# Transposing the gated feed-forward activations between the next pairs of k-tiles, and reloading the spilled ones through another pool of tiles

## The chip, the cores and the metric

The kernel is one program on one core of one Trainium2 chip. The metric is the device time of a whole execution in microseconds (us), the median of several runs. Engines are named as the profile names them: PE is TensorE (matrix products and transposes) and PEld its weight loads, DVE is VectorE, ACT is ScalarE, POOL is GpSimd, and SP is the engine that issues nearly all transfers (DMA).

## What is computed

The reference is one transformer layer on 256 positions of 2048 features, in fp32. Three kinds of attention come first; the part that matters here is the feed-forward block and what stands on either side of it:

```
h = layer_norm(ALPHA * h + mixed @ w_out[i], ln1_g[i], ln1_b[i])
a, b = jnp.split(h @ w_ffn_in[i], 2, axis=-1)
h = layer_norm(ALPHA * h + (jax.nn.silu(a) * b) @ w_ffn_out[i], ln2_g[i], ln2_b[i])
```

Here `h` is 256 x 2048, `w_ffn_in` is 2048 x 11264 (so `a` and `b` have 5632 columns each), and `w_ffn_out` is 5632 x 2048. `silu(a) * b` are the gated activations.

## The kernel before

**Products.** To keep fp32 accuracy each operand is split into a high part and a low remainder (`halves`, L144 on ACT for the high part, L145 on DVE for the low one), and each product is three matmuls: high by high, low by high, high by low. Weights come from HBM in tiles of 512 KB (two k-tiles of 128 rows by 512 columns), are split into `whi` and `wlo`, and feed PE. The 256 positions are two halves of 128, `h` = 0 and 1.

**The gated chunks.** The 5632 columns of the gate are 11 chunks of 512, `c` = 0 to 10. Chunk 0 (`first_chunk`) runs two plain products (`gemm`, matmul lines L212 to L214). Chunks 1 to 10 (`next_chunk`) go through `pair_gemm` (matmul lines L257 to L259), which handles the 16 k-tiles as eight pairs p0 to p7; a plain pair is 24 matmuls. Pairs 2 and 4 (`SEVEN`) use a seven-product form of a 2x2 block product, which needs combinations of the activations that `Forms.put` prepares (L233 to L238, `xs`, `xf`), and four more PSUM banks `m[1]`, `m[5]`, `m[6]`, `m[7]`, used in the order 1, 7, 5, 6. PSUM has two pools of four banks, `acc` and `sc`; a chunk's sums `c[h][j]` take one (`own`), its `m` tiles the other, and the next chunk swaps them. A chunk ends with additions from PSUM (L307), `silu` on ACT (L951) and the multiplication by `b` on DVE (L952; L945 for chunk 0) into a `g` tile, of which pool `gp` has three.

**Transposing.** The next product needs the activations with features on the partitions. `keep_act` calls `to_dmajor` for each half: four PE transposes of 128x128 into one PSUM bank (L335), emptied by ACT (L966), or by ACT and DVE with the split (L144, L145). Chunks 0 and 1 stay on chip (`STAY` is 2). Chunks 2 to 10 go to an HBM buffer `actd` (L968) and come back in `act_first` (L986) while the first column tile of `w_ffn_out` is computed: the load lands in a tile of pool `raw`, is split into two `k4` tiles, and serves four k-tiles. The pool `raw` has three buffers, and the plain products' weight loads (L155) use the same three.

**What sets the order.** The functions are written as Python that emits instructions; a scheduler then decides each engine's own order, so that it need not be the order of the code. Each engine works through its own list strictly in that order, and waits on semaphores. Beside the main stream there is a list of side tasks: generators that `add` puts there and that `tick` moves on by one step. `gemm` and `pair_gemm` call `tick` after each group of weights or pair. A step's `yield n` asks for `n` ticks until the next.

Of the kernel before, what the change touches and what calls it, by code (L numbers as in the profile page):

```python
# [10 lines left out]
F32 = mybir.dt.float32  # L11
# [4 lines left out]
P = 128  # L16
S = 256
# [16 lines left out]
STAY, AHEAD = 2, 1  # L34
# [87 lines left out]
def build(ctx: ExitStack, tc: tile.TileContext, A: dict):  # L122
    nc = tc.nc
    PE, DVE, ACT, POOL = nc.tensor, nc.vector, nc.scalar, nc.gpsimd

    keep = ctx.enter_context(tc.tile_pool(name="keep", bufs=1))
    wp = ctx.enter_context(tc.tile_pool(name="wp", bufs=4))
    k4 = ctx.enter_context(tc.tile_pool(name="k4", bufs=16))
# [13 lines left out]
    def halves(src, hi, lo):  # L142

        ACT.activation(hi, src, AF.Copy)  # L144
        DVE.tensor_sub(lo, src, hi.bitcast(F32))  # L145
# [16 lines left out]
    side, now, newest = [], [0], [None]  # L162

    def add(gen, *after):
        task = {"gen": gen, "after": after, "done": False, "at": 0}
        side.append(task)
        return task
# [11 lines left out]
    def gemm(src, X, kt, w, sizes=(), spare=(), between=None, parts=1):  # L179

        ps = [acc_tile() for _ in range(1 + parts)]
        cols = [[(ps[0][:, :w], slice(0, w))], []]
        for i in range(parts):
            cols[1].append((ps[1 + i][:, :w // parts], slice(i * w // parts, (i + 1) * w // parts)))
        nk = 1
        while nk * 2 * w <= 1024 and nk < 8:
            nk *= 2  # L190
        rest, at = list(sizes), 0
        while at < kt:
            W = []
            sizes = rest.pop(0) if rest else [nk]
            many = len(sizes) > 4
            for g, n in enumerate(sizes):
                n = min(n, kt - at)
                pool = spare[g] if many and g < len(spare) else None
                hi, lo = weight_group(src[:, at:at + n, :], n, w, pool)
                W.append((at, n, hi, lo))  # L200
                at += n
            newest[0] = lo
            for half in range(2):
                if half and not rest and at == kt and between:
                    between(ps)
                c = slice(half * P, (half + 1) * P)
                for o, d in cols[half]:
                    for k0, n, hi, lo in W:
                        for k in range(k0, k0 + n):
                            xh, xl = X(k)  # L210
                            h, l = hi[:, k - k0, d], lo[:, k - k0, d]
                            PE.matmul(o, xh[:, c], h, start=(k == 0), stop=False)  # L212
                            PE.matmul(o, xl[:, c], h, start=False, stop=False)  # L213
                            PE.matmul(o, xh[:, c], l, start=False, stop=(k == kt - 1))  # L214
            tick()
        return ps
# [27 lines left out]

    def pair_gemm(a, b, X, F, kt, pool, banks):

# [5 lines left out]
        hs = [slice(0, P), slice(P, S)]  # L252
        np_, last = kt // 2, max(F.at)

        def product(o, x, w, first=False, stop=False):
            (xh, xl), (h, l) = x, w
            PE.matmul(o, xh, h, start=first, stop=False)  # L257
            PE.matmul(o, xl, h, start=False, stop=False)  # L258
            PE.matmul(o, xh, l, start=False, stop=stop)  # L259

        def split(src, name, pool, n, **kw):
            hi, lo = (pool.tile([P, n, 512], F32R, name=f"w{name}{x}", tag=f"w{name}{x}", **kw) for x in ("hi", "lo"))
            halves(src, hi, lo)
            return [(hi[:, i, :], lo[:, i, :]) for i in range(n)]

        for p in range(np_):
# [3 lines left out]
            x = [[tuple(t[:, hs[h]] for t in X(2 * p + k)) for k in range(2)] for h in range(2)]  # L270
            if p not in F.at:
                w = [split(raw[:, 2:4, :], "", wp, 2), split(raw[:, 0:2, :], "", wp, 2)]
# [18 lines left out]
            product(c[0][0], x[0][1], b21)  # L291
            product(c[0][1], F(p, 3), b22)
            product(m[7], F(p, 2), t3, first, stop)
            product(m[5], F(p, 0), t1, first, stop)
            product(m[6], F(p, 1), t2, first, stop)
# [35 lines left out]
    def to_dmajor(X, k0, src, half, raw=None, bank=None):  # L331

        tp = (bank or sc_tile)()
        for i in range(4):
            PE.transpose(tp[:, i * P:(i + 1) * P], src[:, i * P:(i + 1) * P], ident)  # L335
        tp = tp.rearrange("p (n t) -> p n t", n=4)
        if X is not None:
            X.put(k0, 4, half, tp)
        if raw is not None:
            raw(half, k0, tp)  # L340

    def g_tile():
        return gp.tile([P, 2, 512], F32, name="g", tag="g")
# [480 lines left out]
    dram = ctx.enter_context(tc.tile_pool(name="dram", bufs=9, space=bass.MemoryType.DRAM))  # L824
# [4 lines left out]
    for n in range(4):  # L829
        G = gates(n) if n else G0  # L830
        mix = None
        for name, kt, k0 in (("dsa", 6, 10), ("nsa", 4, 0), ("fox", 6, 4)):
            ps = gemm(A["br_" + name][n], lambda k: O(k0 + k), kt, 512)
            g = G[name]
# [101 lines left out]
    actT = Halves()  # L936

    def first_chunk():
        g = g_tile()
        ps = gemm(A["ffn_in"][0], hT, KT, 512, sizes=[[2] * LONG3], spare=[k4b] * (LONG3 - 4))  # L940
        for h in range(2):
            ACT.activation(g[:, h, :], ps[h], AF.Silu)
        ps = gemm(A["ffn_in"][11], hT, KT, 512)
        for h in range(2):
            DVE.tensor_mul(g[:, h, :], g[:, h, :], ps[h])  # L945
        return [g[:, h, :] for h in range(2)]

    def next_chunk(c, pool, banks):
        e = pair_gemm(A["ffn_in"][c], A["ffn_in"][11 + c], hT, F, KT, pool, banks)
        for h in range(2):  # L950
            ACT.activation(e[h][:, 0, :], e[h][:, 0, :], AF.Silu)  # L951
            DVE.tensor_mul(e[h][:, 0, :], e[h][:, 0, :], e[h][:, 1, :])  # L952
        return [e[h][:, 0, :] for h in range(2)]

    spilled = {}

    def keep_act(c, g, bank):

        if c < STAY:
            actT.add(k4)  # L960
            for h in range(2):
                to_dmajor(actT, 4 * c, g[h], h, bank=bank)
            return
        t = k4.tile([P, 4, S], F32, name="act", tag="k4")
        for h in range(2):
            to_dmajor(None, 4 * c, g[h], h, lambda h, k0, tp: ACT.copy(t[:, :, h * P:(h + 1) * P], tp), bank)  # L966
        spilled[c] = dram.tile([P, 4, S], F32, name="actd")
        nc.sync.dma_start(spilled[c], t)  # L968

    keep_act(0, first_chunk(), acc_tile)  # L970
    part.close()
    with tc.tile_pool(name="fw", bufs=2) as fw:
        F = Forms(k4, SEVEN)
        for p in SEVEN:
            F.put(p, hT)
        for c in range(1, 11):
            banks = (sc_tile, acc_tile) if c % 2 else (acc_tile, sc_tile)
            keep_act(c, next_chunk(c, fw, banks), banks[0])
    k4b = ctx.enter_context(tc.tile_pool(name="k4c", bufs=14))

    def act_first(k):

        for c in range(len(actT.t), min(k // 4 + AHEAD + 1, 11)):
            raw = wp.tile([P, 1024], F32, name="raw", bufs=3)
            raw = raw.rearrange("p (k t) -> p k t", k=4)
            nc.sync.dma_start(raw, spilled[c])  # L986
            actT.add(k4 if c < 4 else k4b)
            halves(raw, *actT.t[c])
        return actT(k)

    later = Later(k4)
    add_and_norm(A["ffn_out"], actT, 44, lambda n: (Y[0][n], Y[1][n]), lambda: params("ln2_g", "ln2_b", k4),
                 lambda: gated_input(k4, 2, k4), later, LONG2, [k4b] * (LONG2 - 4), first=act_first)
    h2T = later.x
    for n in range(4):
# [61 lines left out]
```

## Time and profile before

| what | value |
|---|---|
| median of 3 runs | 1626.53 us (1626.1 to 1627.22) |
| time of the profiled execution | 1622.71 us |
| its span, first to last instruction | 1620.4 us |
| PE busy | 1600.4 us (99%), 7521 matmuls and transposes |
| DVE busy | 1036.8 us (64%) |
| ACT busy | 770.1 us (48%) |
| mean granted TensorE clock | 0.998 |
| bytes moved | 319.71 MB, mean 197 GB/s |

The span is what the trace covers; the profiled execution's own time is 2.3 us longer, for what lies around it, and 3.8 us under the median of the runs. The ends of matmuls are modelled in the trace, so a PE that is shown busy may still be running below its pace; starts of successive matmuls are the better measure.

### The profile page before, as it was taken

To read this page: it belongs to the slowest core of one execution; us is meant where nothing else is said; L and a number is where in the kernel's file an instruction comes from. 1 tells how busy PE (TensorE), PEld (TensorE's weight loads), DVE (VectorE), ACT (ScalarE), POOL (GpSimd) and SP (SyncE) were. 2 spreads that over 40 slices of the span, in tenths; PEclk is the share of its full clock that TensorE was granted. 3 is DMA by queue.
4 is the path that set the end of the run, shared out by engine and by line. 5 is a ranking of instruction groups with operands and counts; after the bars stand their busy time and mean duration, and the time that the engine had idled before them with its cause. 6 is when DMAs were issued, how large, how long until landed. Compare 5 with 4: busy or idle time off the path is not lost. (4 is left out here: it accounts for less than half of the span.)

```text
span 1620.4 us, 19963 instructions
## 1 busy us (share of the span) xinstructions
PE 1600.4 (99%) x7521; PEld 1337.9 (83%) x7521; DVE 1036.8 (64%) x1346; ACT 770.1 (48%) x958; POOL 17.9 (1%) x38
## 2 busy tenths in 40 slices
PE   9999999999999999999999999999999999999998
PEld 7777899988888888888878888888888778888787
DVE  5679765554646454566777777777878555545764
ACT  5455555554444444444455545445555444433443
POOL 1000000010000000000000000000000000000000
PEclk9999999999999999999999999999999999999999
DMA  8665653566666666677565556656566677666474
GB/s 264 191 194 154 206 159 110 167 207 227 189 193 190 194 192 186 194 233 224 163 214 183 192 203 219 211 205 209 207 221 235 201 236 222 193 194 196 152 232 132
DMA packets 92752, 319.71 MB, mean 197 GB/s; under 512 B 10608, under 2 KB 11760, under 8 KB 92656
## 3 DMA queue, kind: packets, MB, share of 16 engines
q1 hardware_dynamic: 91376, 314.25, 61.2%
q0 software_dynamic: 1280, 4.20, 0.9%
q8 instruction: 59, 0.97, 0.2%
q14 instruction: 37, 0.30, 0.1%
HBM read 311.58 MB, written 6.82 MB: 196 GB/s over the span
## 5 line engine op out<-in xcount | busy, mean ns | idle before, releaser
L145 DVE TENSOR_TENSOR wlo<-raw,whi 128x1024 fp32r<-128x1024 f32 (+2 forms) x532 | 633.1, 1193 | 504.6 <-ACT whi L144 499.0
L144 ACT ACTIVATE whi<-raw 128x1024 fp32r<-128x1024 f32 (+2 forms) x532 | 550.4, 1035 | 722.8 <-PE acc L213 372.7
L212 PE MATMUL acc<-whi,k4h 128*128 128x512 f32 (+3 forms) x1580 | 608.3, 385 | 2.1 <-ACT k4h L144 1.6
L214 PE MATMUL acc<-wlo,k4h 128*128 128x512 f32 (+3 forms) x1580 | 602.1, 381 | 3.2 <-DVE wlo L145 3.2
L213 PE MATMUL acc<-whi,k4l 128*128 128x512 f32 (+3 forms) x1580 | 602.0, 381 | 0.6 <-DVE k4l L145 0.6
L212 PEld LDWEIGHTS acc<-whi,k4h 128*128 128x128 f32 x1580 | 297.7, 189 | 56.9 <-ACT k4h L144 2.4
L214 PEld LDWEIGHTS acc<-wlo,k4h 128*128 128x128 f32 x1580 | 297.6, 188 | 56.8 <-DVE wlo L145 5.2
L213 PEld LDWEIGHTS acc<-whi,k4l 128*128 128x128 f32 x1580 | 297.9, 189 | 51.6 <-DVE k4l L145 1.4
L259 PE MATMUL acc<-wlo,k4h 128*128 128x512 f32 x240 | 94.4, 393 | 0.0
L259 PE MATMUL sc<-wlo,k4h 128*128 128x512 f32 x240 | 94.2, 393 | 0.0
L258 PE MATMUL acc<-whi,k4l 128*128 128x512 f32 x240 | 93.6, 390 | 0.0
L257 PE MATMUL sc<-whi,k4h 128*128 128x512 f32 x240 | 93.5, 390 | 0.0
L258 PE MATMUL sc<-whi,k4l 128*128 128x512 f32 x240 | 93.5, 390 | 0.0
L257 PE MATMUL acc<-whi,k4h 128*128 128x512 f32 x240 | 93.5, 389 | 0.0
L258 PEld LDWEIGHTS acc<-whi,k4l 128*128 128x128 f32 x240 | 45.1, 188 | 9.5
L258 PEld LDWEIGHTS sc<-whi,k4l 128*128 128x128 f32 x240 | 45.1, 188 | 9.4
L257 PEld LDWEIGHTS sc<-whi,k4h 128*128 128x128 f32 x240 | 45.1, 188 | 9.1
L259 PEld LDWEIGHTS sc<-wlo,k4h 128*128 128x128 f32 x240 | 45.1, 188 | 9.1
L257 PEld LDWEIGHTS acc<-whi,k4h 128*128 128x128 f32 x240 | 45.1, 188 | 9.1
L259 PEld LDWEIGHTS acc<-wlo,k4h 128*128 128x128 f32 x240 | 45.1, 188 | 9.0
L145 DVE TENSOR_TENSOR wtlo<-raw,wthi 128x1024 fp32r<-128x1024 f32 x40 | 47.9, 1220 | 0.0
L144 ACT ACTIVATE wthi<-raw 128x1024 fp32r<-128x1024 f32 x40 | 41.2, 1046 | 2.4 <-DVE raw L282 2.0
(305 smaller groups left out, 1208.5 us busy)
## 6 DMA issues: line engine op xcount, KB each, us to landing
raw<-ffn_in SPq DMA_DIRECT2D x176, 512.0 KB, 4.5
raw<-gate SPq DMA_DIRECT2D x96, 512.0 KB, 3.6
raw<-ffn_out SPq DMA_DIRECT2D x88, 512.0 KB, 4.3
raw<-att_c SPq DMA_DIRECT2D x40, 512.0 KB, 4.4
raw<-att_f SPq DMA_DIRECT2D x48, 384.0 KB, 3.3
raw<-w_out SPq DMA_DIRECT2D x32, 512.0 KB, 3.7
raw<-ple_gate SPq DMA_DIRECT2D x32, 512.0 KB, 4.4
raw<-cmp SPq DMA_DIRECT2D x16, 512.0 KB, 4.1
```

Of the source, the lines that this page charges most:

```text
L144: ACT.activation(hi, src, AF.Copy)
L145: DVE.tensor_sub(lo, src, hi.bitcast(F32))
L212: PE.matmul(o, xh[:, c], h, start=(k == 0), stop=False)
L213: PE.matmul(o, xl[:, c], h, start=False, stop=False)
L214: PE.matmul(o, xh[:, c], l, start=False, stop=(k == kt - 1))
L257: PE.matmul(o, xh, h, start=first, stop=False)
L258: PE.matmul(o, xl, h, start=False, stop=False)
L259: PE.matmul(o, xh, l, start=False, stop=stop)
```

## The change

`keep_act` becomes a generator with one step for each half. `on_the_side` runs it up to its first `yield` at once (which takes the tiles) and hands the rest to the side list, so that the first half's transposes are emitted at the first `tick` after it, and the second half's at the next. Chunk 0's task is handed over once `F` is made, and `F.put` follows it in the code. The spilled chunks come back into a `g` tile of pool `gp`, not a `raw` tile.

```diff
     def keep_act(c, g, bank):
         if c < STAY:
             actT.add(k4)
-            for h in range(2):
-                to_dmajor(actT, 4 * c, g[h], h, bank=bank)
-            return
-        t = k4.tile([P, 4, S], F32, name="act", tag="k4")
+            put, done = actT, None
+        else:
+            t = k4.tile([P, 4, S], F32, name="act", tag="k4")
+            put, done = None, lambda h, k0, tp: ACT.copy(t[:, :, h * P:(h + 1) * P], tp)
         for h in range(2):
-            to_dmajor(None, 4 * c, g[h], h, lambda h, k0, tp: ACT.copy(t[:, :, h * P:(h + 1) * P], tp), bank)
-        spilled[c] = dram.tile([P, 4, S], F32, name="actd")
-        nc.sync.dma_start(spilled[c], t)
-
-    keep_act(0, first_chunk(), acc_tile)
+            yield 1
+            to_dmajor(put, 4 * c, g[h], h, done, bank)
+        if c >= STAY:
+            spilled[c] = dram.tile([P, 4, S], F32, name="actd")
+            nc.sync.dma_start(spilled[c], t)
+
+    def on_the_side(gen):
+        add(gen)["at"] = now[0] + next(gen)
+
+    g = first_chunk()
     part.close()
     with tc.tile_pool(name="fw", bufs=2) as fw:
         F = Forms(k4, SEVEN)
+        on_the_side(keep_act(0, g, acc_tile))
         for p in SEVEN:
             F.put(p, hT)
         for c in range(1, 11):
             banks = (sc_tile, acc_tile) if c % 2 else (acc_tile, sc_tile)
-            keep_act(c, next_chunk(c, fw, banks), banks[0])
+            on_the_side(keep_act(c, next_chunk(c, fw, banks), banks[0]))
...
-            raw = wp.tile([P, 1024], F32, name="raw", bufs=3)
-            raw = raw.rearrange("p (k t) -> p k t", k=4)
+            raw = g_tile().rearrange("p h (k t) -> p (h k) t", t=S)
             nc.sync.dma_start(raw, spilled[c])
```

First place, PE at the end of chunk 0 and the start of chunk 1. Before, the eight transposes stand after the first product of chunk 1 (the `sc<-whi` rows are its pair p0):

```order
L214 MATMUL acc<-wlo,k4h 128x512
L257 MATMUL sc<-whi,k4h 128x512
L258 MATMUL sc<-whi,k4l 128x512
L259 MATMUL sc<-wlo,k4h 128x512
L335 MATMUL acc<-ident,g 128x128 x8
L257 MATMUL sc<-whi,k4h 128x512
```

With the change four of them stand after the 24 matmuls of pair p0, and the other four after the 24 of pair p1, ahead of the seven-product pair p2 (`wdhi`); the piece shown is the second:

```order
L259 MATMUL sc<-wlo,k4h 128x512
L335 MATMUL acc<-ident,g 128x128 x4
L257 MATMUL acc<-wdhi,k4h 128x512
L258 MATMUL acc<-wdhi,k4l 128x512
L259 MATMUL acc<-wdlo,k4h 128x512
L257 MATMUL sc<-wdhi,k4h 128x512
```

So both sets move behind one and two pairs of independent products. In chunks 2 to 10 both sets stood inside pair p0 before (four transposes, then nine matmuls, then four), and move in the same way.

Second place, PE at the end of chunk 10, where the first column tile of `w_ffn_out` begins (L212 to L214). Before, all eight transposes stand ahead of its first matmul:

```order
L259 MATMUL acc<-wlo,k4h 128x512
L335 MATMUL acc<-ident,g 128x128 x8
L212 MATMUL acc<-whi,k4h 128x512
L213 MATMUL acc<-whi,k4l 128x512
L214 MATMUL acc<-wlo,k4h 128x512
```

With the change the first four stand after the first 12 matmuls of that product (one weight tile), and the second four, shown here with the end of the first 12 ahead of the first four, after 12 more:

```order
L214 MATMUL acc<-wlo,k4h 128x512
L335 MATMUL acc<-ident,g 128x128 x4
L212 MATMUL acc<-whi,k4h 128x512
L213 MATMUL acc<-whi,k4l 128x512
L214 MATMUL acc<-wlo,k4h 128x512
```

Third place, SP's list in the same stretch: `raw<-ffn_out` are weight tiles, `actd<-act` is the last store, and the loads from `actd` bring chunks 2, 3, 4, ... back. Before:

```order
L155 DMA raw<-ffn_out 128x1024 x2
L870 DMA g<-pT 128x512
L986 DMA raw<-actd 128x1024
L155 DMA raw<-ffn_out 128x1024 x2
L986 DMA raw<-actd 128x1024
L155 DMA raw<-ffn_out 128x1024
L968 DMA actd<-act 128x1024
L155 DMA raw<-ffn_out 128x1024
L986 DMA raw<-actd 128x1024
L155 DMA raw<-ffn_out 128x1024 x2
```

With the change:

```order
L155 DMA raw<-ffn_out 128x1024 x2
L992 DMA g<-actd 128x1024
L155 DMA raw<-ffn_out 128x1024 x4
L992 DMA g<-actd 128x1024
L155 DMA raw<-ffn_out 128x1024
L971 DMA actd<-act 128x1024
L992 DMA g<-actd 128x1024
L155 DMA raw<-ffn_out 128x1024
L992 DMA g<-actd 128x1024
L155 DMA raw<-ffn_out 128x1024 x2
```

The loads of spilled chunks no longer stand between the weight loads as users of the same three buffers, and the last store stands ahead of the load of chunk 4 and the ninth weight tile.

ACT's list at the start of chunk 3 shows what the copies of chunk 2's transposes stand behind. Before (`whi_7759` belongs to pair p1, `whi_7835` and `whi_7839` to p3, `whi_7918` to p5, `wthi` to p2):

```order
L144 ACTIVATE whi_7759<-raw8_7752 128x1024
L966 COPY act_7698<-acc_7699 128x4x128
L966 COPY act_7698<-acc_7705 128x4x128
L144 ACTIVATE whi_7835<-raw8_7832 128x1024
L144 ACTIVATE whi_7839<-raw8_7832 128x1024
L144 ACTIVATE wthi_7803<-raw_7791 128x1024
```

With the change:

```order
L144 ACTIVATE whi_7835<-raw8_7832 128x1024
L144 ACTIVATE whi_7839<-raw8_7832 128x1024
L965 COPY act_7698<-acc_7738 128x4x128
L144 ACTIVATE wthi_7803<-raw_7791 128x1024
L965 COPY act_7698<-acc_7779 128x4x128
L144 ACTIVATE whi_7918<-raw8_7915 128x1024
```

Both copies move behind the weights of p3 and stay ahead of those of p5. In chunk 1 alone the second half's copy (`k4h`) moves behind the weights of p5 as well.

## Rows read from the trace of the kernel before

**Rows 1.** The page, busy us, share of the span and instructions by engine:
```profile
PE 1600.4 (99%) x7521; PEld 1337.9 (83%) x7521; DVE 1036.8 (64%) x1346; ACT 770.1 (48%) x958; POOL 17.9 (1%) x38
```

**Rows 2.** Waits of PE, whole span: us in total, times, longest:
```profile
PE acc L335 <- DVE g L952: 3.5, 1, 3.5
PE acc L214 <- DVE wlo L145: 3.2, 3, 2.1
PE acc L335 <- DVE g L945: 2.0, 1, 2.0
```

**Rows 3.** Timeline of PE, chunk 0 to chunk 1: start, us, instruction [idle before]:
```profile
835.66 0.39 PE L259 MATMUL sc<-wlo,k4h 128*128 128x512 f32 x1
838.07 1.25 PE L335 MATMUL acc<-ident,g 128*128 128x128 f32 x8 [2.02 <-DVE g L945]
839.08 0.48 PE L257 MATMUL sc<-whi,k4h 128*128 128x512 f32 x1
```

**Rows 4.** Timeline of PE, chunk 10 to the first product of `w_ffn_out`:
```profile
1269.21 0.39 PE L259 MATMUL acc<-wlo,k4h 128*128 128x512 f32 x1
...
1273.51 0.66 PE L335 MATMUL acc<-ident,g 128*128 128x128 f32 x4 [3.47 <-DVE g L952]
1273.92 0.47 PE L212 MATMUL acc<-whi,k4h 128*128 128x512 f32 x1
...
1278.11 0.39 PE L214 MATMUL acc<-wlo,k4h 128*128 128x512 f32 x1
```

**Rows 5.** Windows: us, busy us by engine, granted clock (after POOL), DMA share, GB/s:
```profile
838.00:840.00 2.00, 1.93 (x12) 1.63 (x13) 2.00 (x4) 1.20 (x2) 0.00 (x0) 1.00 1.02 410
1273.00:1278.00 5.00, 4.49 (x15) 3.63 (x16) 2.22 (x3) 1.67 (x3) 0.00 (x0) 0.66 0.74 188
```

**Rows 6.** Timeline of PE late in the first column tile of `w_ffn_out`:
```profile
1321.68 0.39 PE L214 MATMUL acc<-wlo,k4h 128*128 128x512 f32 x1
...
1323.11 0.50 PE L214 MATMUL acc<-wlo,k4h 128*128 128x512 f32 x1 [0.53 <-DVE wlo L145]
...
1329.83 0.50 PE L214 MATMUL acc<-wlo,k4h 128*128 128x512 f32 x1 [0.53 <-DVE wlo L145]
...
1330.40 0.39 PE L213 MATMUL acc<-whi,k4l 128*128 128x512 f32 x1
```

**Rows 7.** Timeline of SP, two successive loads of spilled chunks:
```profile
1294.38 0.33 SPq L986 DMA_DIRECT2D raw<-actd  x1
...
1301.25 0.33 SPq L986 DMA_DIRECT2D raw<-actd  x1
```

**Rows 8.** DMA issues, 1270 to 1323 us: KB each, median us to landing:
```profile
raw<-ffn_out SPq DMA_DIRECT2D x15, 512.0 KB, 4.2
raw<-actd SPq DMA_DIRECT2D x8, 512.0 KB, 4.3
```

**Rows 9.** Timeline of PE at an ordinary boundary, chunk 2 to chunk 3:
```profile
967.20 0.39 PE L258 MATMUL acc<-whi,k4l 128*128 128x512 f32 x1
...
968.14 0.39 PE L257 MATMUL acc<-whi,k4h 128*128 128x512 f32 x1
...
969.98 0.60 PE L335 MATMUL sc<-ident,g 128*128 128x128 f32 x4
...
975.00 0.39 PE L258 MATMUL acc<-whi,k4l 128*128 128x512 f32 x1
...
978.63 0.39 PE L259 MATMUL acc<-wlo,k4h 128*128 128x512 f32 x1
```

**Rows 10.** Timeline of ACT in chunk 3:
```profile
970.62 0.59 ACT L966 COPY act<-sc 128x512 f32<-128x512 f32 x1 [1.03 <-PE sc L335]
...
981.66 1.06 ACT L144 ACTIVATE whi<-raw 128x1024 fp32r<-128x1024 f32 x1 [6.21 <-DMA raw<-ffn_in]
```

**Rows 11.** DMA issues, 800 to 822 us, in chunk 0:
```profile
raw<-ffn_in SPq DMA_DIRECT2D x15, 512.0 KB, 5.5
```

**Rows 12.** Windows, 800 to 820 us (columns as in rows 5):
```profile
800.00:820.00 20.00, 20.00 (x91) 16.41 (x90) 11.29 (x11) 11.11 (x12) 0.00 (x0) 1.00 0.85 281
```

## The prediction

> **What bounds the kernel now.** The page comes first: PE is busy 99% of the span [rows 1], so only what PE loses can be won, and the list of PE's waits says where that is. The longest there are one wait of 3.5 us and one of 2.0 us, both of a transpose (L335) for the last DVE multiplication of a chunk, and three waits of a matmul for a low part of the weights, 3.2 us together [rows 2]. What stands out is that the transposes wait in two of the eleven chunks only. I then read PE's timeline at those places, and take starts of matmuls, since their ends are modelled.
>
> The pace: between 975.00 and 978.63 us lie 16 intervals, so a matmul starts every 0.227 us when nothing is late [rows 9]. The price of four transposes: from 967.20 to 968.14 us lie two such intervals and one set of four at an ordinary boundary, so a set costs 0.94 - 0.45 = 0.49 us [rows 9]. There the transposes already stand among the next chunk's products, and nothing waits.
>
> **First term, chunk 0 to chunk 1.** From 835.66 to 839.08 us are 3.42 us [rows 3]. The change puts a whole pair of products ahead of each set, so what remains is one matmul and two sets, 0.23 + 0.98 = 1.21 us. That wins 2.2 us. The multiplications L945 are ready when the transposes start at 838.07 us [rows 3]; with the change the first set comes after all 24 matmuls of p0, of which the one at 835.66 us is the third: 835.66 + 22 x 0.227 = 840.7 us, so it waits for nothing.
>
> **Second term, chunk 10 to `w_ffn_out`.** From 1269.21 to 1278.11 us are 8.90 us, in which lie 12 matmul intervals and two sets [rows 4]. At pace these are 12 x 0.227 + 0.98 = 3.70 us. That wins 5.2 us, if the first 24 matmuls of `w_ffn_out` can run while DVE and ACT finish chunk 10. They use chunks 0 and 1, which stayed on chip, and the first two of the three weight tiles that SP's list has ahead of the first reload. [...]
>
> **Third term, the reloads.** For each spilled chunk SP must fetch three tiles of 512 KB, two of weights and the chunk, and PE uses them up in 24 matmuls, 5.45 us. The loads of chunks follow each other at 1294.38 and 1301.25 us, every 6.87 us [rows 7]: three loads through three buffers, each held for 4.2 us of landing [rows 8] and about 2.6 us of splitting on ACT and DVE. So loading loses 1.42 us per chunk, 12.8 us over nine, until its lead is used up. That is where PE stands at 1321.68 to 1330.40 us: 8.72 us for 29 intervals, which at pace are 6.58 [rows 6]. With the chunks in `g` tiles only two loads per 5.45 us go through the three `raw` buffers, so a buffer may be held 8.2 us and is held 6.8. Loading then keeps its lead, and this wins 2.1 us. The `g` tiles also keep up: three of them for one load each 5.45 us.
>
> **What the rest costs.** No instruction is added or dropped, so the rest is about order.
> - The copies from PSUM come a pair later. The second set of a chunk starts at T, its copy starts 0.64 us later (969.98 to 970.62) and takes 0.59 [rows 9, 10], so the bank is empty at T + 1.2 us. The next products are pair p2's, whose `m` tiles come from the same four banks; the first two to be used take the banks that the transposes don't. At the earliest the fourth product needs the last bank, at T + 0.49 + 9 x 0.227 = T + 2.5 us. I take nothing; without that cover it costs 0.6 us and more per chunk.
> - `wthi` of p2 stands behind the first copy on ACT, so DVE's `wtlo` may be later by the copy's 0.59 us; it is needed a whole pair, 5.45 us, later. Nothing.
> - The store of a chunk moves on SP to between the two loads of pair p6, where it waits for the second copy; the loads behind it are for pairs at least three pairs, 16 us, away. Nothing. The last store stands ahead of chunk 4's load and the ninth weight tile. It can go when the second set has been copied, near 1269.4 + 24 x 0.227 + 0.98 + 0.7 = 1276.6 us, and the ninth tile is used after 96 matmuls and two sets, near 1292.2 us. It needs 4.2 us to land and 2.6 to be split. Nothing.
> - `Forms.put` (14 instructions on DVE) moves in the order from the boundary into chunk 0's products. At no more than the 0.59 us of the copy each that is under 8.3 us, and DVE is idle 8.7 of the 20 us there [rows 10, 12]. Weights' low parts can be late by at most one such instruction, and PE has no wait there now. Nothing.
>
> **The sum.** 2.2 + 5.2 + 2.1 = 9.5 us. The profiled execution, 1622.7 us with its 1620.4 us of span, becomes 1613.2 us. It is 3.8 us under the median of the runs; I carry the 9.5 us over to the median: 1626.5 - 9.5 = 1617 us, 0.6% faster. A measurement of this kernel can tell about 0.2% (3.3 us) from no change, so this is about three times that.
>
> **Rivals.**
> *The transfers bind, not the buffers.* Three tiles each 5.45 us are 289 GB/s. Where the trace moves 281 GB/s, in chunk 0, a tile lands in 5.5 us, not 4.2, and the engines' share is 0.85 [rows 11, 12]. With 2.6 us of splitting a buffer is then held 8.1 of the 8.2 us allowed: just enough. If landing rises to 6.1 us, each of the seven rounds of three tiles loses 0.6 us, up to 4.2 us less what lead there is. So the third term lies between the full 2.1 and a loss of 2.1. Against it: 410 GB/s over 2 us [rows 5], and nothing asks for more than 289. It gives 1619 us when the old wait merely stays and 1621 us at the far end. [...]
>
> *The copies come late, and it ends slower.* If ACT reached the second copy of each chunk only behind the weights of p5, it would do so after a load that now ends at 981.66 us [rows 10], two `whi` later, with the bank empty near 984.4 us. The second set would stand near 978.4 us (p1 ends at 978.63 + 0.23 us now, with both sets ahead of it), and p2's sixth product, the last `m` tile, needs a bank by T + 0.49 + 15 x 0.227 = 982.3 us: a wait of 2.1 us in each of ten chunks, 21 us, against 9.5 won: 1638 us. It decides from about 1 us per chunk. In the order the copy is ahead of p5's weights in chunks 2 to 10 and behind them in chunk 1 alone, so one such wait at most is likely: 1619 us.
>
> *The change does nothing at most boundaries, and less than it says at the two.* Nine boundaries had no PE wait to lose. [...] The opposite bound: a set that costs the 0.41 us of 1273.51 to 1273.92 us [rows 4] in place of 0.49 at all 22 sets wins 1.8 us more, 1615 us.
>
> **Chances.** All three terms within 2 us (1615 to 1619): 0.62. Transfers bind (1619 to 1621): 0.15. Late copies in a chunk or two, or half of the second term (1619 to 1623): 0.11. Better than 1615 us: 0.05. No change that can be measured: 0.04. Slower by late copies: 0.03. Faster by over 0.2% (under 1623.3 us) is then 0.91, within 0.2% 0.06 with the edge of the third case, slower 0.03. For 8 in 10 I take the first case whole, 1 us below for the bound on the sets and the runs' own spread, and the transfers' case: 1613.5 to 1621 us.
>
> **What would show it.** Right: no wait of L335 for L945 or L952 in PE's list; granted clock 1.00 over 1265 to 1280 us; loads from `actd` no longer in step with the weights' buffers and ahead of use; no wait for `wlo` in the first tile of `w_ffn_out`; span near 1611 us. Wrong: a wait of L257 for ACT or DVE at the start of pair p2, tiles landing in over 5.5 us between 1270 and 1320 us, or a wait for `wlo` between 805 and 835 us.

## The result, and the profile after

The changed kernel takes 1612.93 us (median of 4 runs, 1611.54 to 1614.24) against 1626.8 us for the kernel before (median of 4 runs, 1626.1 to 1627.22). The ratio is 0.9915, with a 95% interval of 0.9898 to 0.9932, so the change wins 13.9 us, and by the interval between 11 and 17. The forecast was 1617 us, a gain of 9.5, with a range down to 1613.5: the direction and the places were right, and the gain was too small.

The profiled execution of the changed kernel took 1614.24 us with a span of 1612.0 us, so it is one of the slower ones of its kernel, as the profiled one of before was one of the faster. The page's busy times, columns as in [rows 1]:

```profile
PE 1598.5 (99%) x7521; PEld 1338.9 (83%) x7521; DVE 1035.2 (64%) x1346; ACT 768.6 (48%) x958; POOL 16.9 (1%) x38
```

Nothing there tells the two kernels apart; PE's waits do. These are the first of the changed kernel's, columns as in [rows 2]:

```profile
PE sc L537 <- DVE ra L530: 2.3, 1, 2.3
PE acc L214 <- DVE wlo L145: 2.1, 1, 2.1
PE sc L365 <- DVE ones L362: 1.1, 1, 1.1
PE acc L213 <- DVE k4l L145: 1.0, 3, 0.6
```

Both waits of L335, for L945 and for L952, are gone. Of the three waits of L214 for `wlo` one is left, the longest, and it lies at 126 us in the attention stage. PE's timeline at the two boundaries, to be held against [rows 3, 4], and at the end of the first column tile of `w_ffn_out`, against [rows 6]:

```profile
837.26 0.39 PE L257 MATMUL sc<-whi,k4h 128*128 128x512 f32 x1
...
842.47 0.39 PE L259 MATMUL sc<-wlo,k4h 128*128 128x512 f32 x1
842.70 0.60 PE L335 MATMUL acc<-ident,g 128*128 128x128 f32 x4
843.06 0.48 PE L257 MATMUL sc<-whi,k4h 128*128 128x512 f32 x1
...
1268.11 0.39 PE L259 MATMUL acc<-wlo,k4h 128*128 128x512 f32 x1
1268.34 0.39 PE L212 MATMUL acc<-whi,k4h 128*128 128x512 f32 x1
...
1271.06 0.60 PE L335 MATMUL acc<-ident,g 128*128 128x128 f32 x4
1271.41 0.48 PE L212 MATMUL acc<-whi,k4h 128*128 128x512 f32 x1
...
1274.25 0.60 PE L335 MATMUL acc<-ident,g 128*128 128x128 f32 x4
1274.61 0.48 PE L212 MATMUL acc<-whi,k4h 128*128 128x512 f32 x1
...
1328.89 0.39 PE L214 MATMUL acc<-wlo,k4h 128*128 128x512 f32 x1
```

No row has an idle time in brackets. The transposes come 24 matmuls into chunk 1 and 12 and 24 into `w_ffn_out`, and the next product starts 0.35 or 0.36 us behind the start of each set. The tile's 264th matmul starts at 1328.89 us, 60.79 us after the last one of chunk 10; 264 intervals of 0.227 us and two sets are 60.9, so nothing is left to win in this tile. The windows there (columns as in [rows 5]) and the DMA issues of 1270 to 1323 us (columns as in [rows 8]):

```profile
1265.00:1280.00 15.00, 15.00 (x72) 12.44 (x71) 10.83 (x13) 9.11 (x11) 0.00 (x0) 1.00 0.81 261
1270.00:1323.00 53.00, 53.00 (x239) 43.91 (x238) 35.44 (x31) 30.64 (x31) 0.00 (x0) 1.00 0.85 288
```

```profile
raw<-ffn_out SPq DMA_DIRECT2D x19, 512.0 KB, 4.7
g<-actd SPq DMA_DIRECT2D x8, 512.0 KB, 6.6
```

The granted clock is 1.00 where it was 0.66 [rows 5]. The weights' tiles land in 4.7 us where it was 4.2 [rows 8], at 288 GB/s.

So that kernels can be compared by stage, the table below cuts the spans at starts of matmuls in PE's timeline: the first L257 (here 837.26), the last L259 (1268.11) and the 264th matmul behind it (1328.89). The last column names the stop, behind chunk 0 or chunk 10, after which the granted clock fell in that execution. The kernel names are those of the experiments below, and "before" stands there three times, with three profiles.

| kernel | to chunk 1 | chunks 1 to 10 | first tile | rest | span | granted clock falls at a stop |
|---|---|---|---|---|---|---|
| before, shown ahead | 835.20 | 434.01 | 68.23 | 283.00 | 1620.4 | chunk 10 |
| before (x1_before) | 834.88 | 434.83 | 70.01 | 283.03 | 1622.7 | chunk 10 |
| before (x2_before) | 837.39 | 434.39 | 69.41 | 283.37 | 1624.6 | chunk 10 |
| the change | 837.26 | 430.85 | 60.79 | 283.09 | 1612.0 | neither |
| the change (x1_after) | 838.31 | 430.84 | 60.79 | 282.92 | 1612.9 | neither |
| side steps alone (x1_side) | 837.38 | 432.12 | 68.61 | 283.39 | 1621.5 | neither |
| reloads alone (x1_reload) | 835.01 | 436.02 | 63.74 | 284.19 | 1619.0 | chunk 0 |
| chunk 0 as before (x2_first) | 835.46 | 434.77 | 60.79 | 282.93 | 1613.9 | chunk 0 |
| chunk 10 as before (x2_last) | 836.58 | 430.85 | 65.20 | 283.09 | 1615.7 | chunk 10 |
| chunks 1 to 9 as before (x2_mid) | 834.22 | 431.95 | 60.79 | 283.00 | 1610.0 | neither |

Between the two profiles shown first, chunks 1 to 10 win 3.16 us and the first tile 7.44, together 10.6, where the forecast had 2.2 and 5.2 + 2.1. The stage ahead took 2.06 us more, so the spans differ by 8.4 us. Most of the 2.06 is a fall of the clock in the attention stage, (1 - 0.76) x 7 = 1.7 us, that the profile of before does not have there. This is an estimate; where before has its fall behind chunk 10, (1 - 0.66) x 5 = 1.7 us [rows 5] and the starts of matmuls, 1278.11 - 1273.92 - 11 x 0.227 = 1.7 us [rows 4], agree. The window in the changed kernel, then in before:

```profile
40.00:47.00 7.00, 5.47 (x21) 4.73 (x22) 5.69 (x14) 2.89 (x5) 0.80 (x3) 0.76 0.80 260
40.00:47.00 7.00, 5.47 (x29) 4.66 (x30) 5.90 (x14) 3.35 (x6) 0.80 (x3) 1.00 0.84 270
```

A second fall there is in both, to 0.53 at 124 to 127 us in before and at 127 to 130 us in the changed kernel.

### The profile page after: what moved, and what is told of

Same layout as the page of the kernel before. It is cut to its first block, busy times and chain, and to the rows that moved or that the text cites. A ratio compares the mean times of both kernels' runs of the same rounds, so it can differ in the third digit from the quotient of the medians.

```text
span 1612.0 us, 19950 instructions
## 1 busy us (share of the span) xinstructions
PE 1598.5 (99%) x7521; PEld 1338.9 (83%) x7521; DVE 1035.2 (64%) x1346; ACT 768.6 (48%) x958; POOL 16.9 (1%) x38
## 5 line engine op out<-in xcount | busy, mean ns | idle before, releaser
L212 PE MATMUL acc<-whi,k4h 128*128 128x512 f32 (+3 forms) x1580 | 608.1, 385 | 1.2 <-ACT k4h L144 0.7
L214 PE MATMUL acc<-wlo,k4h 128*128 128x512 f32 (+3 forms) x1580 | 601.4, 381 | 2.1 <-DVE wlo L145 2.1
L212 PEld LDWEIGHTS acc<-whi,k4h 128*128 128x128 f32 x1580 | 297.3, 188 | 55.4 <-issue 2.2
L214 PEld LDWEIGHTS acc<-wlo,k4h 128*128 128x128 f32 x1580 | 297.3, 188 | 54.6 <-DVE wlo L145 3.1
L257 PE MATMUL sc<-whi,k4h 128*128 128x512 f32 x240 | 94.0, 391 | 0.0
L257 PE MATMUL acc<-whi,k4h 128*128 128x512 f32 x240 | 93.9, 391 | 0.0
L259 PE MATMUL sc<-wlo,k4h 128*128 128x512 f32 x240 | 93.6, 390 | 0.0
L259 PE MATMUL acc<-wlo,k4h 128*128 128x512 f32 x240 | 93.5, 390 | 0.0
L259 PEld LDWEIGHTS sc<-wlo,k4h 128*128 128x128 f32 x240 | 45.1, 188 | 9.4
L259 PEld LDWEIGHTS acc<-wlo,k4h 128*128 128x128 f32 x240 | 45.1, 188 | 9.4
L257 PEld LDWEIGHTS acc<-whi,k4h 128*128 128x128 f32 x240 | 45.1, 188 | 9.2
L257 PEld LDWEIGHTS sc<-whi,k4h 128*128 128x128 f32 x240 | 45.1, 188 | 9.2
```

## The experiments

### The change in two halves

Two kernels each make one half of the change, and two repeat both ends. x1_side keeps the reload in a `raw` tile and takes the rest of the change; x1_reload is the kernel before with this alone:

```diff
-            raw = wp.tile([P, 1024], F32, name="raw", bufs=3)
-            raw = raw.rearrange("p (k t) -> p k t", k=4)
+            raw = g_tile().rearrange("p h (k t) -> p (h k) t", t=S)
```

Expected of the side steps alone:

> The side steps alone; spilled chunks still come back into raw tiles. Theory A: chunks 1 to 10 as in the changed kernel (430.9 us), the waits of L335 gone, but the waits for wlo late in the first column tile of w_ffn_out stay, since three raw buffers carry three loads for each 5.45 us; that tile takes 63 us, and the median is about 2 us above the changed kernel, 1615 us. Theory B puts no number on it. Rival C (the loads were late only because the long wait let them fall behind): the tile takes 60.8 us and the median is the changed kernel's, 1613 us.

Expected of the reloads alone:

> The reloads into g tiles alone; the transposes stand where they stood before. Theory A: chunks 1 to 10 stay at 434 us, the wait of 3.5 us and the slow clock behind it stay, the waits for wlo late in the first column tile of w_ffn_out go, that tile takes 66 us, and the median falls by 2 us to 1624.5 us. Theory C: the loads' lead is not the buffers' doing, the tile stays at 68 us and the median at 1626.5 us.

Expected of the whole change, once more:

> The changed kernel once more, for a second profile of it and for its time beside the two parts. Theory A: chunks 1 to 10 take 430.9 us, the first column tile 60.8 us, no fall of the granted clock between 830 and 1340 us, median near 1613 us, with a spread of some 2 us that goes with falls of the clock in the attention stage. Theory B: the same median, but a part of the gain over before that neither part alone has.

Expected of the kernel before, once more:

> The kernel before once more, for a second profile of it. Theory A (the change is worth its three waits and a slower clock behind them, and the profiled execution of before was a lucky one): the waits of 2.0 and 3.5 us at the ends of chunks 0 and 10 are there again, chunks 1 to 10 take 434 us and the first column tile of w_ffn_out 68 us, and the granted clock falls in more places than the one at 1273 us and the one near 120 us, one of them behind the wait at 838 us; the median is 1626.5 us. Theory B (the change also removes something that no profile of before has shown): the profile is like the first, near 1620 us of span, and the median is 1626.5 us all the same.

Measured, against the kernel before on the same chip: x1_side 1621.94 us, ratio 0.9967 (0.9955 to 0.9979); x1_reload 1620.93 us, 0.9960 (0.9946 to 0.9974); x1_after 1612.67 us, 0.9911 (0.9896 to 0.9926); x1_before 1626.77 us, 0.9998 (0.9987 to 1.0008). By these ratios of the 1628.0 us that the kernel before took there, the halves win 5.4 and 6.5 us and the whole 14.5. That is 2.6 us more than their sum, but each of the three is known to within 2.0 to 2.4 us only, so that the stages must show it.

The expectations for the halves were missed: the side steps had 1615 us, or 1613 by the rival, and took 1621.94; the reloads had 1624.5 or 1626.5 and took 1620.93. The two ends came out in time as expected, but the profile of x1_before has no fall of the clock behind chunk 0.

The table says where. In x1_side neither boundary has a stop, and the clock stays at 1.00, yet its first tile takes 68.61 us, within the 68.23 to 70.01 of the three profiles of before. The 5.2 us are won at 1270 us and lost again by 1334. Its PE waits from 1262 to 1335 us, then its SP timeline at the loads of spilled chunks (as in [rows 7]), then the last two of the same loads in the changed kernel:

```profile
PE acc L214 <- DVE wlo L145: 3.2, 7, 0.5
PE acc L212 <- ACT whi L144: 0.5, 1, 0.5
```

```profile
1301.28 0.33 SPq L993 DMA_DIRECT2D raw<-actd  x1
...
1307.92 0.33 SPq L993 DMA_DIRECT2D raw<-actd  x1
...
1314.71 0.33 SPq L993 DMA_DIRECT2D raw<-actd  x1
...
1321.38 0.33 SPq L993 DMA_DIRECT2D raw<-actd  x1
```

```profile
1293.79 0.43 SPq L992 DMA_DIRECT2D g<-actd  x1
...
1300.06 0.42 SPq L992 DMA_DIRECT2D g<-actd  x1
```

In x1_side the loads follow each other every 6.6 to 6.8 us, as in [rows 7], and PE uses a chunk up in 5.45, so it waits for a low part of the weights seven times, about once for each load. The idle times are 3.7 us together; with the late starts just behind each, the intervals between matmuls in this tile that are over 0.26 us (but for those at the transposes) come to 7.7 us above 0.227 each, which is nearly the whole of the 7.8 that it takes above the changed kernel's 60.79. In the changed kernel the last spilled chunk is asked for at 1300.06 us, 21 us earlier than in x1_side, and PE waits for none. What the kernel before had at 1270 us was thus one stop that did two things: it cost PE 5.2 us (3.47 of them the wait and 1.7 the clock [rows 4, 5]), and it gave the loads 5.2 us of lead, which held until the waits of [rows 6].

In x1_reload the stop at chunk 10 is there, the clock stays at 1.00 behind it in this execution, and the tile takes 63.74 us with no wait for weights. Against the mean of before's three tiles, 69.2 us, the side steps alone win 0.6 us in this tile, the reloads alone 5.5, and both 8.4. The 5.5 hold some 1.5 us that are not the reloads': behind this stop the clock falls in all three profiles of before, and x2_last below, with the same wait and a fall, takes 65.20 us. At a like clock the reloads alone win about 4.0.

They win part of it by a shorter stop. PE and DVE in x1_reload, then ACT and DVE in the kernel before:

```profile
1274.62 0.66 PE L335 MATMUL acc<-ident,g 128*128 128x128 f32 x4 [2.77 <-DVE g L952]
1272.75 1.22 DVE L145 TENSOR_TENSOR wlo<-raw,whi 128x1024 fp32r<-128x1024 f32 x1
```

```profile
1270.54 1.06 ACT L144 ACTIVATE whi<-raw 128x1024 fp32r<-128x1024 f32 x1 [0.86 <-DMA raw<-ffn_out]
1271.63 1.23 DVE L145 TENSOR_TENSOR wlo<-raw,whi 128x1024 fp32r<-128x1024 f32 x1 [0.61 <-ACT whi L144]
```

On DVE a `wlo` of `w_ffn_out` stands ahead of chunk 10's last multiplication. Before, it waits for ACT's `whi`, and that for a weight tile in the shared buffers; in x1_reload it waits for nothing. So L335 waits 3.45 to 3.89 us in the three profiles of before, and 2.77 in x1_reload and x2_last. The prediction put the whole stop down to the place of the transposes.

x1_side shows one more wait, which the changed kernel has in neither of its profiles, in chunk 1. PE and then ACT there:

```profile
853.75 0.50 PE L257 MATMUL acc<-wthi,xfh 128*128 128x512 f32 x1 [0.97 <-DVE k4l L145]
```

```profile
849.11 2.01 ACT L144 ACTIVATE whi<-raw 128x1024 fp32r<-128x1024 f32 x2 [2.63 <-DMA raw<-ffn_in]
851.02 0.58 ACT L144 ACTIVATE k4h<-acc 128x512 fp32r<-128x512 f32 x1
```

This is the rival of the late copies in the one chunk where it was possible: the second set's copy (`k4h`) stands behind the weights of p5 on ACT, the weights landed late, and the sixth product of p2 waited for the bank. The matmul ahead of it starts 1.36 us earlier, so it cost 1.36 - 0.23 = 1.1 us, where the rival had 2.1 for it.

### One boundary at a time

Three kernels put the transposes of some chunks back to where they stood, in the changed kernel, with `inline` in place of `on_the_side`: chunk 0 in x2_first, chunk 10 in x2_last, chunks 1 to 9 in x2_mid (shown). A fourth is the kernel before.

```diff
+    def inline(gen):
+        for _ in gen:
+            pass
...
-            on_the_side(keep_act(c, next_chunk(c, fw, banks), banks[0]))
+            (on_the_side if c == 10 else inline)(keep_act(c, next_chunk(c, fw, banks), banks[0]))
```

Expected with chunk 0 as before:

> The changed kernel, but chunk 0's eight transposes stand where they stood before; chunks 1 to 10 and the reloads are as changed. Theory: the stop of 2.0 to 2.6 us behind chunk 0 comes back (the earlier runs had 2.41, 2.94, 2.62 us between starts there), and in some executions the granted clock falls behind it, at about 1.7 us each: the median 2.2 to 3.5 us above the changed kernel's, and runs at a clock of 0.998 to 0.999 beside others at 1.00. Rival one, no part of the clock: 2.2 us and no lower clocks than the changed kernel's runs have. Rival two, the whole of the 3.2 us that chunks 1 to 10 win is this stop: 3.2 us even in a profile with no fall of the clock there.

Expected with chunk 10 as before:

> The changed kernel, but chunk 10's eight transposes stand ahead of the first product of the last matrix, as before; the rest is as changed. Theory: the stop of 3 to 3.5 us comes back, with or without a fall of the clock worth 1.7 us, and nothing else, since the reloads into the gate tiles keep ahead either way: the first column tile takes 63.7 us (as with the reload alone) to 66 us in place of 60.8, the median 3 to 5 us above the changed kernel's, no wait of a matmul for a low part of the weights there. Rival: a stop at the start of that tile is time that the reloads need here too, so that part of it was never lost: under 2 us.

Expected with chunks 1 to 9 as before:

> The changed kernel, but chunks 1 to 9 are transposed inside the next chunk's first pair as before; chunks 0 and 10 and the reloads are as changed. Theory: a set of four transposes between two pairs costs about 0.43 us in place of 0.49 inside a pair, so that chunks 1 to 10 take about 1.0 us more (431.9 us in place of 430.85), no new wait: the median 1 us above the changed kernel's. Rival: these nine boundaries had nothing to lose and the 3.2 us of chunks 1 to 10 are all from chunk 0: no difference, 430.9 us.

Expected of the kernel before:

> The kernel before once more, for a second profile beside the first two and for the granted clocks of more runs. Theory: its executions differ by how often the clock falls (each fall about 1.7 us, or 0.001 of the mean clock), so the runs' times follow their mean clock, from about 1622 us at 0.999 to 1628 us at 0.995, and the profile may show a fall behind the wait of chunk 0, which the first two profiles don't. Rival: times differ at one and the same clock, by something else (landing of transfers): no relation between clock and time.

Measured: x2_first 1616.24 us, ratio 0.9939 (0.9923 to 0.9955); x2_last 1617.08 us, 0.9943 (0.9926 to 0.9959); x2_mid 1614.58 us, 0.9928 (0.9912 to 0.9943); x2_before 1627.47 us, 1.0003 (0.9991 to 1.0015). Against the changed kernel's 1612.7 to 1612.9 the first two lose 3.3 to 3.6 and 4.2 to 4.4 us and x2_mid 1.7 to 1.9. These ran on another chip than x1_after; by the ratios, each to its own chip's before, the losses are 3.9 to 4.6, 4.6 to 5.2 and 2.1 to 2.8 us, and a ratio is known to about 2.6 us. So x2_mid's is within what such medians can tell, and the stages decide.

**Chunk 0.** Chunks 1 to 10 take 434.77 us, 3.92 more than in the changed kernel. The transposes' row and a window in x2_first, then the same in x2_before (each in PE's timeline, then in the windows):

```profile
838.40 1.72 PE L335 MATMUL acc<-ident,g 128*128 128x128 f32 x8 [2.10 <-DVE g L945]
```

```profile
838.00:842.00 4.00, 3.60 (x13) 3.04 (x14) 3.89 (x7) 1.19 (x2) 0.00 (x0) 0.59 1.02 396
```

```profile
840.61 1.25 PE L335 MATMUL acc<-ident,g 128*128 128x128 f32 x8 [2.38 <-DVE g L945]
```

```profile
837.00:842.00 5.00, 2.62 (x16) 1.87 (x15) 5.00 (x7) 2.70 (x4) 0.00 (x0) 1.00 0.78 277
```

In x2_first the clock is 0.59 over the 4 us behind a wait of 2.10 us, and matmuls start 0.43 us apart (at 840.34, 840.77 and 841.20 us) in place of 0.227; (1 - 0.59) x 4 = 1.6 us are lost by it, and the other 2.3 of the 3.92 are the stop. In x2_before the wait is longer, 2.38 us, and the clock stays 1.00. The rival of a 3.2 us stop without the clock falls, and by this profile so does that of no part of the clock: the five profiles that have this stop show a fall behind it in two (x1_reload and x2_first). The clocks of the runs do not show it: x2_first's six have 0.998 and 0.999, with the same mean of 0.9987 as the changed kernel's nine.

**Chunk 10.** PE and a window in x2_last:

```profile
1271.03 1.12 PE L335 MATMUL acc<-ident,g 128*128 128x128 f32 x4 [2.77 <-DVE g L952]
```

```profile
1270.00:1275.00 5.00, 3.97 (x13) 3.36 (x14) 3.34 (x4) 1.82 (x3) 0.00 (x0) 0.66 0.99 380
```

The tile takes 65.20 us, 4.41 above the changed kernel's: (1 - 0.66) x 5 = 1.7 us of clock, and 2.7 of the stop. No wait for weights comes with it. So with the reloads out of the `raw` buffers the stop here was a plain loss, and the rival of under 2 us falls.

**Chunks 1 to 9.** They take 431.95 us, 1.10 more than in the changed kernel, as expected, but only partly for the reason that was given. From the start of the matmul ahead of a set to that of the seventh behind it, less seven intervals of 0.227 us, a set costs 0.47 us between pairs, and 0.50 for the first and 0.47 for the second inside a pair; the 0.43 us of the expectation was a misreading, since the matmuls behind a set start 0.230 us apart for a while, in place of 0.227, and a count that stops sooner misses that. Nine first sets at 0.03 are 0.3 us. Most of the rest is short waits at two boundaries; one of them in x2_mid:

```profile
1093.97 0.66 PE L335 MATMUL acc<-ident,g 128*128 128x128 f32 x4 [0.24 <-DVE g L952]
```

That set costs 0.92 us in place of 0.50, and the one two chunks later 0.74. In the kernel before the same two chunks, 6 and 8, give 0.80 and 0.58 us.

**The kernel before.** On average its executions follow their mean granted clock. Its 63 runs beside the experiments (but for one each at 0.994 and 0.995) and the changed kernel's 9, median us and number of runs:

| mean granted clock | before | the change |
|---|---|---|
| 1.000 | none | 1610.5 (1) |
| 0.999 | 1623.9 (7) | 1612.6 (4) |
| 0.998 | 1625.3 (20) | 1613.9 (4) |
| 0.997 | 1627.6 (18) | none |
| 0.996 | 1628.5 (16) | none |

The expected fall behind chunk 0's wait in this profile was not there; x2_first's profile has it. At one and the same clock the change wins 11.3 to 11.4 us, and its runs have a mean clock of 0.9987 against 0.9972 for the 63 runs of before. A straight line through those 63 gives 1.4 us for each 0.001, so the clock adds about 2 us. But runs at one clock lie up to 6.5 us apart (1621.53 to 1628.03 at 0.998), so the rival is not gone: something else moves them too.

## Why the prediction came out too small

**First term, 2.2 us: right.** The stop behind chunk 0 is gone and costs 2.3 us where it is put back; in the three profiles of before it cost 2.4 to 2.9. Its first set waits for nothing, at 842.70 us.

**Second and third terms, 5.2 and 2.1 us: the mechanisms right, the split wrong.** Their sum is 7.3 us and the two profiles differ by 7.44 in that tile. But they are no two terms. The reloads' loss was sized by the two waits that PE had left in one execution [rows 6], and most of what they cost lay hidden behind the stop of the second term. By themselves the side steps win 0.6 us there, and the reloads about 4.0 at a like clock. A part of the second term, 0.7 us of its wait of 3.47, was the reloads' too.

**Costs taken as nothing: right, with one exception in one kernel.** The copy of chunk 3's second set starts 0.6 us behind its transposes and ahead of p5's weights, on ACT in the changed kernel:

```profile
973.02 0.57 ACT L965 COPY act<-sc 128x512 f32<-128x512 f32 x1
...
978.58 0.59 ACT L965 COPY act<-sc 128x512 f32<-128x512 f32 x1 [4.04 <-PE sc L335]
```

`L257` waits for nothing at the start of any p2, and `wlo` for nothing in chunk 0, so `Forms.put` and the store did no harm. (The rows of [rows 9, 10] are of this boundary too, from chunk 3 to chunk 4: chunk 1 starts at 835.20 us there, and a chunk takes 43.4.) The wait in chunk 1 of x1_side shows that chunk 1 has little room. How often the changed kernel meets it is open; neither of its two profiles has it.

**"Nine boundaries had no PE wait to lose": nearly.** Chunks 1 to 9 lose 0.3 us by the place of the first set and 0.1 to 0.5 at each of two chunks.

**The transfers** were no bound. At 288 GB/s a weight tile lands in 4.7 us, so with the forecast's 2.6 of splitting, an estimate (ACT's 1.06 and DVE's 1.23 us above are 2.3, without the gaps around them), a buffer is held 7.3 of the 8.2 us. The landing took longer than in the kernel before, 4.7 us for 4.2 and for the chunks 6.6 for 4.3 [rows 8], while 288 GB/s were moved from 1270 to 1323 us in place of 229; it stayed within the lead. The chunks' 6.6 us is over the 5.5 that the prediction named as a sign of being wrong, and cost nothing: PE waits for none of them. In that rival a round loses 6.1 + 2.6 - 8.2 = 0.5 us, not 0.6, so at most 3.7 and not 4.2; nothing rests on it.

**The step that failed** is "I carry the 9.5 us over to the median". The profiled execution of before was one of the lightest of its kernel, 3.8 us under its median (of the 63 runs above, two are faster), and its waits were sized as if every execution had them so. Two more profiles of before have first tiles of 70.01 and 69.41 us in place of 68.23, and chunks 1 to 10 of 434.83 and 434.39 in place of 434.01: on average of the three 1.4 us more is lost in the parts that the change mends. The chunks' short waits and the sets' places add 0.7. The clock adds the last part: the forecast's 5.2 us hold one fall, behind chunk 10, 1.7 us [rows 4, 5], while a fall behind chunk 0 as well is seen in two of five profiles with that stop, 0.7 us on average. Neither of the two is of the kernel before itself, so this part is an estimate. 9.5 + 1.4 + 0.7 + 0.7 = 12.3 us. The remaining 1.6 us lies within the interval of the measured gain and stays open. Falls of the clock in the attention stage do not explain it as far as the profiles show: the three of before have one there each, the two of the change two each. Nor does the clock elsewhere: at one and the same mean clock the change wins 11.3 to 11.4 us, where the terms without the clock are 9.5 - 1.7 + 1.4 + 0.7 = 9.9; with four runs of the change at each clock, that is a hint. The range had no term for heavier executions: its lower end was for cheaper sets and the runs' spread, and stands 1.5 us below the first case, not the 1 us that it names.

## What to carry to other kernels

A stall gives lead to whatever is bound behind it (here 5.2 us to the loads), so waits that follow each other are not summed: take the earlier one away in thought, run the later stage at its own rate (here 6.6 to 6.8 us against 5.45 for each chunk), and see where its lead runs out. Before a gain is carried from one profile to a median, look at where that execution stands among the runs, and in its granted clock; when it is one of the light ones, its waits are a lower bound.

## What was not expected of the hardware

Stops of much the same length did not always lower the clock here: behind an idle of 2.10 us it fell to 0.59 over 4 us in x2_first, behind 2.38 us in x2_before it stayed 1.00, and behind the wait of 2.77 us at chunk 10 it stayed 1.00 in x1_reload and fell to 0.66 in x2_last. The windows of x1_reload, behind chunk 0, where it fell, and at chunk 10:

```profile
838.00:844.00 6.00, 5.92 (x23) 4.72 (x24) 6.00 (x11) 1.20 (x2) 0.00 (x0) 0.72 1.01 386
1270.00:1276.00 6.00, 3.23 (x19) 2.58 (x18) 5.51 (x7) 4.55 (x7) 0.00 (x0) 1.00 0.73 264
```

So these stops of 2.10 to 2.77 us cost their length in some executions and their length and 1.6 to 1.7 us more in others. These pairs are of different kernels, alike at the place; the kernel before has the fall behind chunk 10 in all three of its profiles and behind chunk 0 in none. Two profiles of before also differ in where the fall begins. At chunk 10 the first still has 1.00 after the transposes' start at 1273.51 us; x2_before has 0.50 already ahead of theirs at 1276.49:

```profile
1273.60:1274.40 0.80, 0.80 (x6) 0.76 (x7) 0.80 (x1) 0.20 (x1) 0.00 (x0) 1.00 0.72 205
1275.90:1276.40 0.50, 0.00 (x0) 0.00 (x0) 0.50 (x2) 0.11 (x1) 0.00 (x0) 0.50 0.07 25
```

PE's idle time was not the only cost of a stop here, then, and a single profile of a stop shows only one of the two prices.
